# Scores of the first 128 queries as three products of rounded parts, in place of one product in full fp32

## The chip, the cores and the metric

The kernel runs on one core of one Trainium2 chip. A core has five engines that work side by side: TensorE (in the profile PE, with its weight loads as PEld), VectorE (DVE), ScalarE (ACT), GpSimd (POOL) and SyncE (SP). The metric is the device time of one execution in microseconds, taken as the median of several runs.

## The reference

The model is a trunk of two layers over 256 positions of 2048 features, with 32 heads of 128. The first layer (A) attends in chunks with a bias by relative distance, the second (B) to a shared key and value stream with a decay that forget gates set. Both have the same shape: a projection to queries, keys, values and a gate, scores, softmax, the weighted sum of the values, the gate, a projection back, a residual. The part that matters here, of layer B:

```python
for i in range(s // Q_BLOCK):               # Q_BLOCK = 128, s = 256
    q0 = i * Q_BLOCK
    end = q0 + Q_BLOCK
    sc = jnp.einsum('bqhd,bkhd->bhqk', q[:, q0:end], k[:, :end]).astype(jnp.float32) * scale
    decay = cum_logf_h[:, :, q0:end, None] - cum_logf_h[:, :, None, :end]
    causal = (q0 + jnp.arange(Q_BLOCK))[:, None] >= jnp.arange(end)[None, :]
    sc = jnp.where(causal[None, None], sc + decay, NEG_INF)
    p = jax.nn.softmax(sc, axis=-1).astype(v.dtype)
    outs.append(jnp.einsum('bhqk,bkhd->bqhd', p, v[:, :end]))
```

So the first 128 queries have scores with the first 128 keys alone, the other 128 queries with all 256. In layer A a chunk of 64 frames sees its own and the chunks before it, which the kernel computes in the same two blocks of 128 queries with a bias of -1e30 where nothing is seen. All is in fp32.

## The kernel before

**Products.** A product of fp32 values is made in one of two ways. In full fp32 it is one call of `pe.matmul`, which the profile shows as two matmul records and two weight loads. The other way splits both operands into a high part, rounded to the type `fp32r`, and a low part, the rounded remainder (`hi` and `lo`), and adds up three products: high by high, high by low, low by high. Every one of these is one record with one load. The large projections work so (`mm3`, L162: lines 164 to 166 are the three products of 512 columns), and so do most products of the attention (`dot3`, L330: lines 331 to 333).

**Order.** The weights of the projections come in blocks of 256 rows by 512 columns. `Feed` (L172) loads them by SP's queue, rounds the high part on ACT (L204) and takes the difference on DVE (L205). It keeps four blocks ready ahead of PE. The heads go in 16 groups of two in each layer, so there are 32 groups. For each group PE runs two units of eight blocks (`aqk` and `avg` in layer A, `bqg` and `bkv` in layer B), and the attention of a group is a generator (`attention`, L335) of which one piece is issued after a given block of the units that follow (`QK_STEPS` and its like; `drive`, L505). Instructions of an engine run in the order in which they are issued, and the buffers of tiles with the same tag are shared in turn, so that a new tile waits for the readers of the old one.

**Attention of one group.** The rows of q and k are transposed in squares of 32 on DVE and moved to their places by 16 DMAs that POOL issues (`turn`, L303). The tile that comes out, `qkZ` in the profile, has the features on the partitions. Then, as pieces of their own:

- `split` (L319) makes high and low parts on ACT (L326) and DVE (L327): of k for all 256 positions (`wideh`, `widel`), of q for the last 128 alone (`q1h`, `q1l`). The first 128 positions of q are copied in fp32 by ACT (L345) into `q0`, which takes the buffer of `oT`.
- The scores: `s1p`, the last 128 queries with all 256 keys, as three products per head with 256 columns each (L350, L351); and `s0p`, the first 128 queries with the first 128 keys, as one product in full fp32 per head with 128 columns (L353).
- Scale and bias on DVE (L360), the maximum (L361), the exponential on ACT (L363), first for `s1p`, then for `s0p`; then the gates are scaled, all is transposed again (`sgZ`), split (`wideh`, `widel` again), and multiplied with the values (`op`, L385 and L386).

At the start a few matmuls on a tile of zeros keep PE busy while the first data come (`heat`, L89).

Of the kernel before, what the change touches and what calls it, by code (L numbers as in the profile page):

```python
# [9 lines left out]
F32 = mybir.dt.float32  # L10
F32R = mybir.dt.float32r
BF16 = mybir.dt.bfloat16
AF = mybir.ActivationFunctionType
# [3 lines left out]
P = 128  # L17
S = 256
# [14 lines left out]
HG = 2  # L33
NG = H // HG
GC = HG * DH
UN = 512
KB = 2
SQ = 32
# [17 lines left out]
def r32(ap):  # L56
    return ap.bitcast(F32)
# [3 lines left out]
def trunk(ctx, tc, x, x_t, gains, a_w_in, a_rel, a_w_out, kv_w, f_w, f_b, b_w_in, b_w_out, final_norm, out):  # L61
    nc = tc.nc
    pe, act, dve, pool, sp = nc.tensor, nc.scalar, nc.vector, nc.gpsimd, nc.sync

    const = ctx.enter_context(tc.tile_pool(name="const", bufs=1))
    big = ctx.enter_context(tc.tile_pool(name="big", bufs=16))
    stream = ctx.enter_context(tc.tile_pool(name="stream", bufs=3))
    att = ctx.enter_context(tc.tile_pool(name="att", bufs=1))
# [5 lines left out]
    def bank(name):  # L74
        return ps_at.tile([P, 512], F32, name=name, tag="at")
# [12 lines left out]

    def heat(n):  # L89

        z = const.tile([P, P + UN], BF16, name="zeros")
        dve.memset(z, 0.0)
        ps = bank("heat")
        for i in range(n):
            pe.matmul(ps, z[:, :P], z[:, P:], start=i == 0, stop=i == n - 1)

    heat(HEAT)
    GA, GKV, GB = 0, KD, 2 * KD

# [203 lines left out]
    def turn(src, n, name):  # L303

        y = att.tile([P, NQ, n, SQ], F32, name=f"{name}Y", tag="Y")
        dve.transpose(y, src.rearrange("p n (j u) -> p j n u", u=SQ))  # L308
        z = att.tile([P, NQ, n, SQ], F32, name=f"{name}Z", tag="Z")
        for i in range(NQ):  # L310
            for j in range(NQ):
                pool.dma_start(out=z[j * SQ:(j + 1) * SQ, i], in_=y[i * SQ:(i + 1) * SQ, j])  # L312
        return z
# [2 lines left out]
        for t in range(NT):  # L316
            act.activation(dst[:, t], acc[t][:, c0:c1], AF.Copy, scale=rs[:, t:t + 1])

    def split(srcs, tag):  # L319

        n, nt = len(srcs), srcs[0].shape[1]
        hi = att.tile([P, n, nt * P], F32R, name=f"{tag}h", tag=f"{tag}h")
        lo = att.tile([P, n, nt * P], F32R, name=f"{tag}l", tag=f"{tag}l")
        for k, src in enumerate(srcs):
            h, l = (v[:, k].rearrange("p (t i u) -> p t i u", t=nt, u=SQ) for v in (hi, lo))
            act.activation(h, src, AF.Copy)  # L326
            dve.tensor_sub(l, src, r32(h))  # L327
        return hi, lo

    def dot3(out_, a, b, stop=True):  # L330
        pe.matmul(out_, a[0], b[0], start=True, stop=False)
        pe.matmul(out_, a[0], b[1], start=False, stop=False)
        pe.matmul(out_, a[1], b[0], start=False, stop=stop)

    def attention(g, biases, qk, vg, half, ocat):  # L335


        z = turn(qk.rearrange("p t (c d) -> p (t c) d", d=DH), NT * 2 * HG, "qk")
        bias1, bias0 = biases()
        qkT = z.rearrange("p i (t c) u -> p c t i u", t=NT)  # L340
        yield
        kh, kl = split([qkT[:, HG + i] for i in range(HG)], "wide")
        qh, ql = split([qkT[:, i, 1:] for i in range(HG)], "q1")
        q0 = att.tile([P, HG, P], F32, name="q0", tag="oT")
        act.activation(q0.rearrange("p h (i u) -> p h i u", u=SQ),  # L345
                       qkT[:, :HG, 0], AF.Copy)
        yield
        s1p = bank("s1p")[:, :].rearrange("p (i s) -> p i s", i=HG)
        s0p = bank("s0p")[:, :HG * P].rearrange("p (i s) -> p i s", i=HG)
        for i in range(HG):  # L350
            dot3(s1p[:, i], (qh[:, i], ql[:, i]), (kh[:, i], kl[:, i]))  # L351
        for i in range(HG):
            pe.matmul(s0p[:, i], q0[:, i], qkT[:, HG + i, 0], start=True, stop=True)  # L353
        NB = 1 + NT
        sg = att.tile([P, HG * NB + NT * HG, P], F32, name="sg", tag="R")
        sv = sg[:, :HG * NB].rearrange("p (i c) k -> p i (c k)", i=HG)
# [11 lines left out]
        c = small.tile([P, NT, HG], F32, name="csc")  # L368
# [7 lines left out]
        z = turn(sg, HG * NB + NT * HG, "sg")  # L376
        pT = z[:, :, :HG * NB].rearrange("p i (h c) u -> p h c i u", h=HG)
        gT = z[:, :, HG * NB:].rearrange("p i (t h) u -> p h t i u", t=NT)
        yield
        ph, pl = split([pT[:, i, :NT] for i in range(HG)], "wide")  # L380
        yield
        op = bank("op").rearrange("p (i s) -> p i s", i=HG)
# [5 lines left out]
        oT = att.tile([P, HG, S], F32, name="oT", tag="oT")  # L388
# [4 lines left out]
        lo = ocat.lo[h0 // BIG][:, h0 % BIG:h0 % BIG + HG, :]  # L393
# [87 lines left out]
    def side_a(g, accs):  # L481
        tb = att.tile([P, HG, S], F32, name="tb", tag="tb")
        for lo_, hi_, c0 in ((0, CHUNK, CHUNK), (CHUNK, P, 0)):
            sp.dma_start(out=tb[lo_:hi_, :, c0:], in_=bass.AP(
                tensor=a_rel.tensor, offset=a_rel.offset + g * HG * NREL + REL + 1 - P + lo_ + c0,
                ap=[[1, hi_ - lo_], [NREL, HG], [1, S - c0]]))

        def biases():
            pool.memset(tb[:CHUNK, :, :CHUNK], NEG)
            return tb[:, :, ::-1], tb[:, :, P - 1::-1]  # L490

        qk = rows(UN, "qk")
        evac_scaled(accs["qk"], 0, UN, rsA, qk)
        yield

        def vg():
            return accs["v"], accs["g"]

        yield from attention(g, biases, qk, vg, halfA, oA)
# [272 lines left out]
```

## Time and profile before

| | |
|---|---|
| median of 3 runs | 1859.43 us (1858.83 to 1859.74) |
| profiled execution | 1860.0 us |
| its span, first to last instruction | 1858.3 us |
| mean granted clock of TensorE | 0.996 |
| busy: PE, PEld | 1840.2 us, 1525.3 us |
| busy: DVE, ACT, POOL | 1123.8 us, 1008.2 us, 542.6 us |

A row of the profile that groups instructions has the line of the kernel, the engine, the operation, the tile written and the tiles read, the shape, the count, then the busy time in us, the mean duration of one in ns, and the engine's idle time before them with what ended it. `128*128 128x256` on a matmul is the size of the weights, then partitions by columns that stream. A row in order of time has the start in us, the duration in us, engine, line and operation; several alike are merged with their count, and the duration is then from the first start to the last end. A row of waits has who waited, for whom, the sum in us, how often, and the longest. A row by stretches of time has the stretch, its length, the busy time and count of PE, PEld, DVE, ACT and POOL, the granted clock, the share of the DMA engines and GB/s.

A matmul's record is as long as it takes from its start to its last result, and the next one starts before that. The time from one start to the next is therefore read from the order of time.

### The profile page before, as it was taken

The numbers are of one execution on the slowest core, as the hardware profiler recorded it, in microseconds if no ns is written. First come the engines' busy times: TensorE is split into PE (matmuls) and PEld (weight loads), VectorE is DVE, ScalarE is ACT, GpSimd is POOL, SyncE is SP. The second block draws the span as 40 slices with busy tenths as digits, with TensorE's granted clock in tenths as the row PEclk, the third lists the DMA queues.
The fourth block names the chain that finished last, engine by engine and source line by source line (L and its number), as shares of the span: only waits on it lengthen the run. The fifth ranks groups of instructions, "written<-read, shape, count | busy, mean of one in ns | idle before, by whom it ended". The sixth has DMA issues, their size and how long they took to land.

```text
span 1858.3 us, 25119 instructions
## 1 busy us (share of the span) xinstructions
PE 1840.2 (99%) x8395; PEld 1525.3 (82%) x8395; DVE 1123.8 (60%) x1450; ACT 1008.2 (54%) x1688; POOL 542.6 (29%) x1129
## 2 busy tenths in 40 slices
PE   8999999999999999999999999999999999999998
PEld 6888888888888888887888888888888888888886
DVE  6666656666666666555665666666665665655554
ACT  5555555555555555545555555555555655554443
POOL 0433333333333333111103333333333333333000
PEclk9999999999999999999999999999999999999999
DMA  8666666666676666666767666666666666676664
GB/s 281 216 216 210 212 214 219 214 208 217 215 212 210 217 215 212 208 218 222 230 185 220 209 216 215 216 217 213 214 214 218 214 213 213 212 235 214 207 203 161
DMA packets 141970, 398.43 MB, mean 214 GB/s; under 512 B 31088, under 2 KB 35472, under 8 KB 141456
## 3 DMA queue, kind: packets, MB, share of 16 engines
q1 hardware_dynamic: 106816, 356.35, 60.3%
q0 software_dynamic: 34304, 39.39, 6.6%
q8 instruction: 67, 1.10, 0.2%
q10 hardware_dynamic: 720, 1.07, 0.2%
q14 instruction: 63, 0.52, 0.1%
HBM read 353.15 MB, written 4.23 MB: 192 GB/s over the span
## 4 chain that ended last, share of the span: by engine, by line
PE 88%; DMA 5%; DVE 2%; POOL 2%; ACT 2%; issue 1%; SPq 0%; ACTq 0%; POOLq 0%; DVEq 0%
PE avg_acc L164 6%; PE bqg_acc L164 6%; PE bqg_acc L166 6%; PE bqg_acc L165 6%; PE avg_acc L165 6%; PE avg_acc L166 6%; PE bkv_acc L164 5%; PE bkv_acc L165 5%; PE bkv_acc L166 5%; PE aqk_acc L166 5%; PE aqk_acc L164 5%; PE aqk_acc L165 5%; PE bo_acc L166 3%; PE bo_acc L165 3%; PE bo_acc L164 3%; DMA sgZ<-sgY 2%
## 5 line engine op out<-in xcount | busy, mean ns | idle before, releaser
L312 POOL DMA_DIRECT2D sgZ<-sgY x512 | 250.5, 497 | 467.9 <-DVE sgY L308 410.1
L312 POOL DMA_DIRECT2D qkZ<-qkY x512 | 251.0, 497 | 379.4 <-DVE vl L405 97.3
L205 DVE TENSOR_TENSOR avg_lo<-avg_raw,avg_hi 128x1024 fp32r<-128x1024 f32 x128 | 156.5, 1223 | 130.3 <-ACT avg_hi L204 130.2
L205 DVE TENSOR_TENSOR bqg_lo<-bqg_raw,bqg_hi 128x1024 fp32r<-128x1024 f32 x128 | 156.6, 1223 | 129.4 <-ACT bqg_hi L204 129.4
L204 ACT ACTIVATE bqg_hi<-bqg_raw 128x1024 fp32r<-128x1024 f32 x128 | 135.4, 1058 | 143.2 <-PE bqg_acc L166 85.1
L204 ACT ACTIVATE avg_hi<-avg_raw 128x1024 fp32r<-128x1024 f32 x128 | 135.3, 1057 | 141.3 <-PE avg_acc L166 84.0
L205 DVE TENSOR_TENSOR aqk_lo<-aqk_raw,aqk_hi 128x1024 fp32r<-128x1024 f32 (+1 forms) x129 | 155.3, 1211 | 88.3 <-ACT aqk_hi L204 88.2
L164 PE MATMUL aqk_acc<-aqk_hi,xTh 128*128 128x512 f32 x512 | 202.2, 396 | 3.3 <-ACT xTh L142 3.0
L205 DVE TENSOR_TENSOR bkv_lo<-bkv_raw,bkv_hi 128x1024 fp32r<-128x1024 f32 x128 | 155.3, 1219 | 77.0 <-ACT bkv_hi L204 76.7
L166 PE MATMUL aqk_acc<-aqk_hi,xTl 128*128 128x512 f32 x512 | 200.6, 392 | 1.1 <-DVE xTl L143 1.1
L165 PE MATMUL aqk_acc<-aqk_lo,xTh 128*128 128x512 f32 x512 | 200.6, 392 | 1.1 <-DVE aqk_lo L205 1.1
L164 PE MATMUL bkv_acc<-bkv_hi,xkvh 128*128 128x512 f32 x512 | 201.1, 393 | 0.0
L164 PE MATMUL avg_acc<-avg_hi,xTh 128*128 128x512 f32 x512 | 200.7, 392 | 0.0
L164 PE MATMUL bqg_acc<-bqg_hi,xbh 128*128 128x512 f32 x512 | 200.7, 392 | 0.0
L166 PE MATMUL bqg_acc<-bqg_hi,xbl 128*128 128x512 f32 x512 | 199.5, 390 | 0.0
L166 PE MATMUL bkv_acc<-bkv_hi,xkvl 128*128 128x512 f32 x512 | 199.5, 390 | 0.0
L166 PE MATMUL avg_acc<-avg_hi,xTl 128*128 128x512 f32 x512 | 199.4, 389 | 0.0
L165 PE MATMUL bqg_acc<-bqg_lo,xbh 128*128 128x512 f32 x512 | 199.3, 389 | 0.0
L165 PE MATMUL avg_acc<-avg_lo,xTh 128*128 128x512 f32 x512 | 199.3, 389 | 0.0
L165 PE MATMUL bkv_acc<-bkv_lo,xkvh 128*128 128x512 f32 x512 | 199.2, 389 | 0.0
L204 ACT ACTIVATE aqk_hi<-aqk_raw 128x1024 fp32r<-128x1024 f32 (+1 forms) x129 | 134.8, 1050 | 86.2 <-PE aqk_acc L166 46.0
L204 ACT ACTIVATE bkv_hi<-bkv_raw 128x1024 fp32r<-128x1024 f32 x128 | 134.6, 1057 | 72.8 <-PE bqg_acc L166 41.9
(193 smaller groups left out, 3451.8 us busy)
## 6 DMA issues: line engine op xcount, KB each, us to landing
avg_raw<-in_a_w_in SPq DMA_DIRECT2D x128, 512.0 KB, 4.2
bqg_raw<-in_b_w_in SPq DMA_DIRECT2D x128, 512.0 KB, 4.2
bkv_raw<-in_kv_w SPq DMA_DIRECT2D x128, 512.0 KB, 4.2
aqk_raw<-in_a_w_in SPq DMA_DIRECT2D x127, 512.0 KB, 4.1
ao_raw<-in_a_w_out SPq DMA_DIRECT2D x64, 512.0 KB, 4.3
bo_raw<-in_b_w_out SPq DMA_DIRECT2D x64, 512.0 KB, 4.1
sgZ<-sgY POOLq DMA_DIRECT2D x512, 40.0 KB, 3.9
qkZ<-qkY POOLq DMA_DIRECT2D x512, 32.0 KB, 3.6
```

The costliest lines, as they stand in the source:

```text
L164: pe.matmul(acc[t], lhs.h(k)[:, ts], hi, start=k == 0, stop=False)
L165: pe.matmul(acc[t], lhs.h(k)[:, ts], lo, start=False, stop=False)
L166: done.append(pe.matmul(acc[t], lhs.l(k)[:, ts], hi, start=False, stop=k == nk - 1))
L204: act.activation(hi[:, j], raw[:, j], AF.Copy)
L205: self.splits.append(dve.tensor_sub(lo[:, j], raw[:, j], r32(hi[:, j])))
L312: pool.dma_start(out=z[j * SQ:(j + 1) * SQ, i], in_=y[i * SQ:(i + 1) * SQ, j])
```

## The change

The scores of the first 128 queries are made like those of the last: three products of rounded parts for each head, with 128 columns. For this, q is split over all its 256 positions (`qh`, `ql`), and the fp32 copy `q0` goes. The first 128 columns of the rounded q and k serve `s0p`, the last 128 of q and all of k serve `s1p`. The low part of q takes the buffer of `oT`, where `q0` was (`split` has an argument for it), and the zeros of the warm-up take the buffer of the gates, `gs`, in place of one of their own.

```diff
     def heat(n):
-        z = const.tile([P, P + UN], BF16, name="zeros")
+        z = att.tile([P, P + UN], BF16, name="zeros", tag="gs")
...
-    def split(srcs, tag):
+    def split(srcs, tag, low=None):
         n, nt = len(srcs), srcs[0].shape[1]
         hi = att.tile([P, n, nt * P], F32R, name=f"{tag}h", tag=f"{tag}h")
-        lo = att.tile([P, n, nt * P], F32R, name=f"{tag}l", tag=f"{tag}l")
+        lo = att.tile([P, n, nt * P], F32R, name=f"{tag}l", tag=low or f"{tag}l")
...
         kh, kl = split([qkT[:, HG + i] for i in range(HG)], "wide")
-        qh, ql = split([qkT[:, i, 1:] for i in range(HG)], "q1")
-        q0 = att.tile([P, HG, P], F32, name="q0", tag="oT")
-        act.activation(q0.rearrange("p h (i u) -> p h i u", u=SQ),
-                       qkT[:, :HG, 0], AF.Copy)
+        qh, ql = split([qkT[:, i] for i in range(HG)], "q", "oT")
         yield
...
-        for i in range(HG):
-            dot3(s1p[:, i], (qh[:, i], ql[:, i]), (kh[:, i], kl[:, i]))
-        for i in range(HG):
-            pe.matmul(s0p[:, i], q0[:, i], qkT[:, HG + i, 0], start=True, stop=True)
+        for s_, t, n in ((s1p, 1, S), (s0p, 0, P)):
+            for i in range(HG):
+                dot3(s_[:, i], *((h[:, i, c], l[:, i, c]) for h, l, c in
+                                 ((qh, ql, slice(t * P, (t + 1) * P)), (kh, kl, slice(0, n)))))
```

## The prediction

> **What bounds the kernel now.** I read the head of the profile page first, then the waits of PE, then the busy time by stage.
>
> ```profile
> span 1858.3 us, 25119 instructions
> PE 1840.2 (99%) x8395; PEld 1525.3 (82%) x8395; DVE 1123.8 (60%) x1450; ACT 1008.2 (54%) x1688; POOL 542.6 (29%) x1129
> ...
> PE 88%; DMA 5%; DVE 2%; POOL 2%; ACT 2%; issue 1%; SPq 0%; ACTq 0%; POOLq 0%; DVEq 0%
> ```
>
> ```profile
> PE aqk_acc L164 <- ACT xTh L142: 3.0, 1, 3.0
> ...
> PE aqk_acc L165 <- DVE aqk_lo L205: 1.1, 3, 0.5
> ...
> PE ao_acc L165 <- DVE ao_lo L205: 0.8, 1, 0.8
> PE op L331 <- ACT wideh L326: 0.6, 2, 0.3
> ...
> PE cp L626 <- DVE f_l L615: 0.2, 1, 0.2
> ```
>
> ```profile
> 45.00:750.00 705.00, 704.65 (x3238) 586.27 (x3237) 431.63 (x550) 383.88 (x641) 244.61 (x509) 1.00 0.68 213
> ...
> 1000.00:1690.00 690.00, 689.28 (x3176) 574.51 (x3175) 425.95 (x539) 399.82 (x720) 247.10 (x510) 1.00 0.68 216
> ```
>
> PE is busy for 1840.2 of 1858.3 us. Its waits fill nine rows (the first, the last and the three that a later step needs are shown), all small, and none belongs to the scores. In the two long stretches that hold nearly all of the attention, the first number after the length is PE's busy time: 704.65 of 705 us and 689.28 of 690. The granted clock there is 1.00. So every nanosecond that the change adds to or takes from the PE's stream moves the end by as much, and work on the other engines counts only where it makes PE wait.
>
> A busy PE may hide slow and quick instructions alike, since a record's duration (275 ns for a product of 128 columns) is a latency that overlaps the next record. What counts is the pitch: the time from one record's start to the next one's. So the rest is read from the order of time, and the first question is which of the two pipelined streams, weight loads (PEld) or matmuls (PE), sets that pitch.
>
> **What the edited products cost now.** These are records by form, and then the last of the 32 groups of two heads in order of time.
>
> ```profile
> L353 PE MATMUL s0p<-qkZ,q 128*128 128x128 f32 x128 | 19.6, 275 | 0.0
> ...
> L353 PEld LDWEIGHTS s0p<-qkZ,q 128*128 128x128 f32 x128 | 17.1, 191 | 0.0
> L331 PEld LDWEIGHTS s1p<-wideh,q1h 128*128 128x128 f32 x64 | 12.2, 190 | 1.3
> ...
> L332 PEld LDWEIGHTS s1p<-widel,q1h 128*128 128x128 f32 x64 | 12.2, 190 | 1.2
> ...
> L590 PEld LDWEIGHTS zp<-xkvl,fwh 128*32 128x32 f32 x16 | 1.7, 108 | 0.1
> ```
>
> ```profile
> 1693.92 0.39 PE L164 MATMUL bo_acc<-bo_hi,oBh 128*128 128x512 f32 x1
> ...
> 1694.60 0.28 PE L331 MATMUL s1p<-wideh,q1h 128*128 128x256 f32 x1
> ...
> 1695.31 0.61 PE L353 MATMUL s0p<-qkZ,q 128*128 128x128 f32 x4
> 1695.68 0.47 PE L164 MATMUL bo_acc<-bo_hi,oBh 128*128 128x512 f32 x1
> 1695.99 0.39 PE L165 MATMUL bo_acc<-bo_lo,oBh 128*128 128x512 f32 x1
> ```
>
> There are 64 full-fp32 products (32 heads in two layers) and 128 records: each product is two matmuls with two loads. From 1693.92 three matmuls of 512 columns (L164, L165, L166) go by until 1694.60, so one takes 0.227 us. Six products of rounded parts with 256 columns take from 1694.60 to 1695.31: 0.71/6 = 0.118 us each. From the first fp32 record to L165 are 0.68 us; without the 0.227 us of the L164 between them, 0.453 us is left for four records, 0.113 us each, 0.227 us for a product.
>
> Is this 0.113 us the matmul's or the load's? The cumulative sum of the gates answers that, with six fp32 records of only 32 columns against 128-wide weights:
>
> ```profile
> 973.67 0.38 PE L626 MATMUL cp<-f_l,triu 128*128 128x32 f32 x2 [0.17 <-DVE f_l L615]
> 973.88 0.39 PE L626 MATMUL cp<-f_l,ones 128*128 128x32 f32 x2
> 974.11 0.39 PE L626 MATMUL cp<-f_l,triu 128*128 128x32 f32 x2
> 974.33 0.48 PE L164 MATMUL bkv_acc<-bkv_hi,xkvh 128*128 128x512 f32 x1
> ```
>
> ```profile
> 973.64 0.30 PEld L626 LDWEIGHTS cp<-f_l,triu 128*128 128x128 f32 x2 [0.56 <-issue]
> ...
> 974.30 0.19 PEld L164 LDWEIGHTS bkv_acc<-bkv_hi,xkvh 128*128 128x128 f32 x1
> ```
>
> Six records take 0.66 us, six loads 0.66 us: 0.110 us each, although only a quarter as many columns stream as in s0p. A load of 128 fp32 weights thus takes about 0.110 us of its own stream. The durations agree: 190 ns for 128 weights and 108 ns for 32 make (190 - 108)/96 = 0.85 ns a weight, 109 ns for 128, and the loads of rounded weights (L331 and L332 of s1p) last as long as those of fp32. A narrow product on its own weights therefore can't have a pitch below the load's.
>
> **The change part by part.**
>
> (1) The products. Two fp32 products of a group (four records, 0.453 us) give way to two times three products of rounded parts: six records, each with a load of 128 weights. `dot3` uses the high part of q twice in a row, but s1p does so today, and both lines there have 64 loads of their own, so all six loads stay. The trace has no rounded product with fewer than 256 columns, so its pitch must be bounded. From below: if the matmul's stream alone set it, by the slope (0.227 - 0.118)/256 = 0.426 ns a column, it is 0.118 - 128 x 0.426 = 0.064 us. From above: half the columns should not take longer than the 0.118 us of the 256-wide product, as long as the rate per column holds. I take 0.112 us, the row of the gates and of s0p itself, because these have the same load and no longer stream than it; the 0.064 us would need a load quicker than any of this size in the trace. That makes 2 records more at 0.112 us, +0.224 us a group and +7.2 us over 32 groups. By 0.118 us all six take 0.708 us, +0.255 us a group, +8.2 us; by 0.064 us they take 0.384 us, -0.069 us a group, -2.2 us.
>
> The Trainium skill, "TensorE: Matmul & The Clock Gate", section "Back-to-back issue gap", speaks against this: it gives 81 ns for each matmul of 128 columns in a stream of load and matmul pairs. By that figure six would take an estimated 0.486 us and the change would cost only 1.1 us in all; the trace's 0.110 us with 32 columns disagrees.
>
> (2) The splits. Both heads' q is now rounded over 256 columns and not 128, and the copy at L345 goes.
>
> ```profile
> L326 ACT ACTIVATE wideh<-qkZ 128x256 fp32r<-128x256 f32 x64 | 23.3, 410 | 69.7 <-DMA qkZ<-qkY 69.7
> ...
> L326 ACT ACTIVATE q1h<-qkZ 128x128 fp32r<-128x128 f32 x64 | 15.8, 294 | 0.0
> ...
> L345 ACT ACTIVATE q<-qkZ 128x256 f32<-128x256 f32 x32 | 12.8, 402 | 0.0
> ```
>
> ```profile
> L327 DVE TENSOR_TENSOR widel<-qkZ,wideh 128x256 fp32r<-128x256 f32 x64 | 24.4, 421 | 45.1 <-ACT wideh L326 45.1
> ...
> L327 DVE TENSOR_TENSOR q1l<-qkZ,q1h 128x128 fp32r<-128x128 f32 x64 | 15.6, 285 | 0.0
> ```
>
> ACT: 2 x (410 - 294) - 402 = -170 ns a group. DVE: 2 x (421 - 285) = +272 ns a group, 8.7 us in all on an engine that is 60% busy. The low part is ready 0.27 us later. What covers it is the distance to the product that reads it. In the group with the least distance but one, and in the first:
>
> ```profile
> 240.21 0.49 DVE L327 TENSOR_TENSOR q1l<-qkZ,q1h 128x128 fp32r<-128x128 f32 x2
> ...
> 243.84 0.28 PE L333 MATMUL s1p<-wideh,q1l 128*128 128x256 f32 x1
> ```
>
> ```profile
> 58.51 0.49 DVE L327 TENSOR_TENSOR q1l<-qkZ,q1h 128x128 fp32r<-128x128 f32 x2
> ...
> 59.00 0.28 PE L333 MATMUL s1p<-wideh,q1l 128*128 128x256 f32 x1
> ```
>
> In the fifth group the low parts end at 240.70 and are read at 243.84, over 3 us later. The other 30 have more. Only the first group has them done (59.00) as the PE gets there; I put down 0.2 us, once. Queued behind the longer split on DVE are the low parts of the next weight blocks (L205), four blocks ahead of PE; they take up 0.27 us, since PE waits for such a part only in the first blocks and by 0.8 us in the first output projection. If that cover were gone everywhere, it would cost 32 x 0.27 = 8.7 us.
>
> (3) Later readers and buffers. The scores of the first 128 queries end 0.22 us later. Their reader comes late anyway:
>
> ```profile
> 1697.92 0.41 DVE L360 SCALAR_TENSOR_TENSOR sg<-s0p,d 128x256 f32<-128x256 f32 x1
> ```
>
> It starts 1.9 us after the PE has left s0p (1695.99), since DVE does the other 128 queries first. The low part of q takes the buffer of oT, as q0 did, so it waits for the same readers of the group before; the zeros of the warm-up move into the buffer of the gates, which nothing writes before the first group's second unit is done. No DMA is added or moved, and the transposed tile comes free earlier. All this: 0. The two waits of op (0.6 us) may grow by what the exponentials come later, at most 0.3 us each.
>
> **The sum.** +7.2 + 0.2 = +7.4 us. The profiled run took 1860.0 us (span 1858.3 and 1.7 around it): 1867.4. The median, 1859.43, is 0.6 below that run, which gives 1866.8 us, +0.4%. Its own range runs from 1865.8 (all six at the 0.109 us of the durations: 0.654 us, +0.201 us a group, +6.4 us, and no stall) to 1868.4 (0.118 us: +8.2, the first group's 0.2 and 0.6 for op).
>
> **The rivals.**
>
> A, loads hidden. If rounded weights come through faster than fp32 ones when matmuls are short, the stream sets the pitch: 0.064 us, -2.2 us, 1857.2. For it: at 256 and 512 columns nothing shows that rounded loads hinder. Against: their durations equal those of fp32 weights (190 and 191 ns). It decides below a pitch of 0.453/6 = 0.0755 us; there the change stops costing, and up to (0.453 + 3.7/32)/6 = 0.095 us it stays within 0.2%. The 81 ns of the Trainium skill would fall between these two points and make it 1860.5.
>
> B, passes count. If the price is the array's passes, three replace four: 0.227/4 = 0.057 us less a product, x64 = -3.6 us, 1855.8. The Trainium skill, "FP8 and Floating Point Precision", section "TensorE Precision Notes", counts four passes for true FP32. Against it stands L626: a quarter of the columns at the same pitch.
>
> C, narrow rounded products lose their rate. If under 256 columns each costs what a full-fp32 product does (0.227 us), six take 1.36 us, +0.91 us a group, +29.0 us: 1888.4. Nothing in the trace speaks for or against, since all its rounded products have 256 or 512 columns.
>
> D, the change doesn't do what it says: the repeated high part of q isn't loaded again, four loads as now, no change, 1859.6. Against: the 64 loads on each of the lines 331 and 332.
>
> E, the late split starves PE in all groups: +7.2 + 8.7, 1875.3. Against: the 3 us of cover.
>
> **How the numbers follow.** The forecast 0.74; A 0.10, B 0.04, C 0.06, D 0.03, E 0.03. From 1865.8 to 1868.4 leaves 0.26 out, so the range goes on to A and D: 1857.0 to 1869.0, with 0.13 outside. Of no change I speak up to 0.2%, 3.7 us, about what a measurement of this kernel can tell. Slower are the forecast, C and E, 0.83; A, D and most of B are within it, 0.14; the rest of B, faster, 0.03.
>
> **What would show it.** Right: 192 records of s0p with 192 loads of 128x128, in order of time 0.90 us from the first of them to L165 (now 0.68), PE busier by some 7 us, its waits still about 9, L345 gone from ACT and DVE's splits of q 8.7 us longer. Wrong: a pitch near 0.07 (A) or 0.23 (C), 128 loads (D), or a wait of PE for a split of q beyond the first group (E). A pitch of 0.112 with no longer time would mean that PE isn't the bound, and my reading of its busy time fails.

## The result and the profile after

The changed kernel takes 1870.96 us (median of 4 runs, 1867.66 to 1875.45); the kernel before takes 1859.13 us beside it (4 runs, 1857.07 to 1859.74). The ratio is 1.0065, with a 95% interval from 1.0051 to 1.0078. So the change makes the kernel slower, as forecast, but by about 12 us and not by 7.4, and the median lies above the range (the lowest of its four runs, 1867.66 us, lies in it). The profiled execution took 1872.6 us with a span of 1870.8 us, 12.5 us more than the span before.

The head of the profile page, and the first and the last row of PE's waits (who waited, for whom, sum in us, times, longest):

```profile
span 1870.8 us, 25069 instructions
PE 1848.3 (99%) x8459; PEld 1535.1 (82%) x8459; DVE 1137.7 (61%) x1450; ACT 1003.6 (54%) x1656; POOL 544.0 (29%) x1129
...
PE 90%; DMA 3%; DVE 2%; POOL 2%; issue 1%; ACT 1%; SPq 0%; ACTq 0%; POOLq 0%; DVEq 0%
```

```profile
PE op L331 <- ACT wideh L326: 5.1, 4, 2.2
...
PE cp L623 <- DVE f_l L612: 0.2, 1, 0.2
```

PE is still the bound. It has 64 records more and is busy for 8.1 us more. The wait that has grown most is that of `op`, the product of the exponentials with the values, for the high part of its transposed weights: from 0.6 us in 2 waits to 5.1 us in 4. The one at the start for `xTh` grew from 3.0 to 4.4 us, while some small ones fell. All rows of PE's waits add up to 13.2 us, against 9.0 before.

The records of the edited part by form:

```profile
L331 PE MATMUL s0p<-wideh,qh 128*128 128x128 f32 x64 | 15.9, 248 | 0.0
...
L333 PEld LDWEIGHTS s0p<-wideh,ql 128*128 128x128 f32 x64 | 12.3, 192 | 0.0
...
L327 DVE TENSOR_TENSOR ql<-qkZ,qh 128x256 fp32r<-128x256 f32 x64 | 24.1, 417 | 0.0
...
L326 ACT ACTIVATE qh<-qkZ 128x256 fp32r<-128x256 f32 x64 | 22.7, 402 | 0.0
```

The change does what it says. Each of the lines 331 to 333 has 64 records of 128 columns for `s0p`, and each has 64 loads of its own.

**What a group costs where nothing disturbs it.** PE's records in order of time (start, duration in us), after the change, from the scores of one group to those of the next:

```profile
1333.55 0.28 PE L331 MATMUL s1p<-wideh,qh 128*128 128x256 f32 x1
...
1334.27 0.22 PE L331 MATMUL s0p<-wideh,qh 128*128 128x128 f32 x1
...
1334.89 0.45 PE L164 MATMUL bkv_acc<-bkv_hi,xkvh 128*128 128x512 f32 x1
1335.17 0.39 PE L165 MATMUL bkv_acc<-bkv_lo,xkvh 128*128 128x512 f32 x1
...
1337.67 0.39 PE L164 MATMUL bkv_acc<-bkv_hi,xkvh 128*128 128x512 f32 x1
...
1379.68 0.28 PE L331 MATMUL s1p<-wideh,qh 128*128 128x256 f32 x1
```

And the same view of the kernel before, for the same group:

```profile
1325.92 0.28 PE L331 MATMUL s1p<-wideh,q1h 128*128 128x256 f32 x1
...
1326.63 0.61 PE L353 MATMUL s0p<-qkZ,q 128*128 128x128 f32 x4
...
1327.31 0.39 PE L165 MATMUL bkv_acc<-bkv_lo,xkvh 128*128 128x512 f32 x1
...
1329.85 0.39 PE L164 MATMUL bkv_acc<-bkv_hi,xkvh 128*128 128x512 f32 x1
...
1371.86 0.28 PE L331 MATMUL s1p<-wideh,q1h 128*128 128x256 f32 x1
```

From the first record of `s0p` to L165 it is now 0.90 us (1334.27 to 1335.17), before 0.68 us: the forecast's +0.22. But the whole period of the group grows from 45.94 us (1325.92 to 1371.86) to 46.13 us (1333.55 to 1379.68), by only 0.19 us. The rest was in the matmuls that follow: the eleven from L165 on took 2.54 us before (1327.31 to 1329.85) and take 2.50 us now (1335.17 to 1337.67). After the full-fp32 records the next wide matmuls ran a little slower, and after these six rounded ones they don't. It isn't fp32 alone that makes them slower: after four rounded records, and after two, the same eleven take 2.52 us (the runs with two products and with one, below). What does is open. Over 32 groups 0.187 us (the difference before rounding, mean of the undisturbed groups) make 6.0 us.

**Where the other 6.5 us are.** The first score product of each group marks the time. The records of `s1p<-wideh,qh` in each layer (count, minimum, median and maximum duration in ns, first and last start in us; the last is the second head of the last group), of the kernel before and then of the changed one:

```profile
L331 PE MATMUL s1p<-wideh,q1h x32: 277/280/283, 58.8 to 751.4; 128*128 128x256 f32 x32
...
L331 PE MATMUL s1p<-wideh,q1h x32: 277/280/283, 1003.3 to 1695.0; 128*128 128x256 f32 x32
```

```profile
L331 PE MATMUL s1p<-wideh,qh x32: 277/280/283, 60.2 to 754.8; 128*128 128x256 f32 x32
...
L331 PE MATMUL s1p<-wideh,qh x32: 277/280/283, 1005.3 to 1707.1; 128*128 128x256 f32 x32
```

| stretch | before | after | difference |
|---|---|---|---|
| start to the first score | 58.8 | 60.2 | +1.4 |
| layer A, first to last score | 692.6 | 694.6 | +2.0 |
| to the first score of layer B | 251.9 | 250.5 | -1.4 |
| layer B, first to last score | 691.7 | 701.8 | +10.1 |
| to the end | 163.3 | 163.7 | +0.4 |

Fifteen periods in each layer should cost 15 x 0.187 = 2.8 us more. Layer A has less than that, layer B 7.3 us beyond it. There it sits in two of its groups: the second to start in layer B takes 50.67 us and the thirteenth 50.32 us, where before they took 46.97 and 46.99 us. So 46.13 is exceeded by 4.5 and 4.2 us, 45.94 was exceeded by 1.0 each. Here is what PE does at the end of the first of the two, in order of time (in brackets the idle time and what ended it), and by stretches (length, busy time and count of PE, PEld, DVE, ACT, POOL, then the granted clock):

```profile
1074.36 0.39 PE L166 MATMUL bkv_acc<-bkv_hi,xkvl 128*128 128x512 f32 x1
1076.94 0.39 PE L331 MATMUL op<-wideh,vh 128*128 128x256 f32 x1 [2.19 <-ACT wideh L326]
...
1079.75 0.63 PE L165 MATMUL bqg_acc<-bqg_lo,xbh 128*128 128x512 f32 x1
```

```profile
1074.56:1077.97 3.41, 1.15 (x5) 0.66 (x5) 0.76 (x2) 1.50 (x3) 0.00 (x0) 1.00 0.16 61
1077.97:1081.38 3.41, 3.41 (x12) 3.01 (x13) 3.21 (x5) 2.72 (x7) 0.00 (x0) 0.50 0.23 67
```

PE waits 2.19 us for the split of the transposed exponentials. At 1077.97, 1.03 us after the wait has ended, the granted clock falls to 0.50 for 3.41 us, and the wide matmul at 1079.75 lasts 0.63 us where it otherwise takes 0.39. (In the other group it falls 0.45 us after the wait, and the last section says what the two have in common.) At half speed 3.4 us do the work of 1.7. So the wait costs nearly twice its length, and PE's busy time hides the second half of it.

**Why `op` waits.** DVE in the same group, before and then after, from the scores to the transposition of the exponentials (`sgY`):

```profile
1050.23 0.69 DVE L360 SCALAR_TENSOR_TENSOR sg<-s1p,cb 128x512 f32<-128x512 f32 x1 [1.18 <-PE s1p L333]
1050.84 0.41 DVE L360 SCALAR_TENSOR_TENSOR sg<-s0p,d 128x256 f32<-128x256 f32 x1
1051.17 1.00 DVE L361 TENSOR_REDUCE nm<-sg 128x2 f32<-128x512 f32 x2
1052.09 1.21 DVE L205 TENSOR_TENSOR bkv_lo<-bkv_raw,bkv_hi 128x1024 fp32r<-128x1024 f32 x1
...
1055.89 1.51 DVE L308 STREAM_TRANSPOSE sgY<-sg 128x1280 f32<-128x1280 f32 x1
```

```profile
1052.42 0.69 DVE L357 SCALAR_TENSOR_TENSOR sg<-s1p,cb 128x512 f32<-128x512 f32 x1 [1.19 <-PE s1p L333]
1053.03 1.22 DVE L205 TENSOR_TENSOR bkv_lo<-bkv_raw,bkv_hi 128x1024 fp32r<-128x1024 f32 x1
1054.16 0.68 DVE L358 TENSOR_REDUCE nm<-sg 128x2 f32<-128x512 f32 x1
1054.76 0.41 DVE L357 SCALAR_TENSOR_TENSOR sg<-s0p,d 128x256 f32<-128x256 f32 x1
...
1058.89 1.51 DVE L308 STREAM_TRANSPOSE sgY<-sg 128x1280 f32<-128x1280 f32 x1
```

Before, both scores and both maxima came in one piece. Now the low part of a weight block (L205, 1.22 us) stands between the first score and the first maximum, and the second score comes after that. No line of the diff says so: the planner, which lays the order of DVE's instructions, laid it anew for the changed program, in all 16 groups of layer B. (Before, only the last of them had this order. In layer A the order changed too, to score, maximum, score, maximum, but with no weight part between, and there the transposition starts 5.67 us after the first score in nearly all groups, as before.) The transposition starts 6.47 us after the first score (1052.42 to 1058.89), not 5.66 us (1050.23 to 1055.89). Then 16 transfers follow, issued by POOL, and the rounding on ACT. That rounding in the same group, before and after:

```profile
1072.20 0.72 ACT L326 ACTIVATE wideh<-sgZ 128x256 fp32r<-128x256 f32 x2 [4.17 <-DMA sgZ<-sgY]
```

```profile
1076.47 0.72 ACT L326 ACTIVATE wideh<-sgZ 128x256 fp32r<-128x256 f32 x2 [6.06 <-DMA sgZ<-sgY]
```

It comes 24.05 us after the first score and not 21.97. PE, on the other hand, arrives at `op` 22.33 us after it (1076.94 - 2.19 - 1052.42). Of the 2.08 us that were lost, 0.81 are DVE's; the other 1.27 came up behind it: 0.53 until POOL had issued the last of the transfers, where it waits for earlier ones of the same tile, and 0.74 from there to the rounding. POOL's issues in order of time, after:

```profile
1065.40 4.40 POOL L312 DMA_DIRECT2D sgZ<-sgY  x9 [2.72 <-issue]
1070.13 0.50 POOL L312 DMA_DIRECT2D sgZ<-sgY  x1 [0.33 <-DMA sgZ<-sgY]
1071.40 0.50 POOL L312 DMA_DIRECT2D sgZ<-sgY  x1 [0.77 <-DMA sgZ<-sgY]
```

The gap of 2.72 us in POOL's issues is there in the kernel before as well (2.75 us in this group); both kernels have such a gap, of 2.7 to 3.3 us, in the `sgZ` transfers of four groups out of 32, and these two are among them. All four already exceeded the 45.94 us before, by 0.6 to 1.0 us, and exceed 46.13 us now, the two in layer A by 1.0 and 1.4 us. So it is in these groups above all that the slack runs out.

### The profile page after: what moved, and what is told of

The parts are those of the page before. It is cut to its first block, busy times and chain, and to the rows that moved or that the text cites. A ratio compares the mean times of both kernels' runs of the same rounds, so it can differ in the third digit from the quotient of the medians.

```text
span 1870.8 us, 25069 instructions
## 1 busy us (share of the span) xinstructions
PE 1848.3 (99%) x8459; PEld 1535.1 (82%) x8459; DVE 1137.7 (61%) x1450; ACT 1003.6 (54%) x1656; POOL 544.0 (29%) x1129
## 4 chain that ended last, share of the span: by engine, by line
PE 90%; DMA 3%; DVE 2%; POOL 2%; issue 1%; ACT 1%; SPq 0%; ACTq 0%; POOLq 0%; DVEq 0%
PE avg_acc L164 6%; PE avg_acc L166 6%; PE avg_acc L165 6%; PE bqg_acc L164 6%; PE bqg_acc L165 6%; PE bqg_acc L166 6%; PE aqk_acc L164 5%; PE aqk_acc L166 5%; PE aqk_acc L165 5%; PE bkv_acc L164 5%; PE bkv_acc L166 5%; PE bkv_acc L165 5%; PE ao_acc L165 3%; PE bo_acc L164 3%; PE ao_acc L164 3%; PE ao_acc L166 3%
## 5 line engine op out<-in xcount | busy, mean ns | idle before, releaser
L205 DVE TENSOR_TENSOR avg_lo<-avg_raw,avg_hi 128x1024 fp32r<-128x1024 f32 x128 | 156.4, 1223 | 131.3 <-ACT avg_hi L204 131.0
L205 DVE TENSOR_TENSOR bqg_lo<-bqg_raw,bqg_hi 128x1024 fp32r<-128x1024 f32 x128 | 156.6, 1223 | 130.5 <-ACT bqg_hi L204 130.4
L205 DVE TENSOR_TENSOR aqk_lo<-aqk_raw,aqk_hi 128x1024 fp32r<-128x1024 f32 (+1 forms) x129 | 156.2, 1215 | 92.9 <-ACT aqk_hi L204 92.8
L164 PE MATMUL aqk_acc<-aqk_hi,xTh 128*128 128x512 f32 x512 | 201.9, 395 | 5.0 <-ACT xTh L142 4.4
L164 PE MATMUL bqg_acc<-bqg_hi,xbh 128*128 128x512 f32 x512 | 201.5, 394 | 0.0
L165 PE MATMUL aqk_acc<-aqk_lo,xTh 128*128 128x512 f32 x512 | 200.6, 392 | 0.8 <-DVE aqk_lo L205 0.8
L164 PE MATMUL avg_acc<-avg_hi,xTh 128*128 128x512 f32 x512 | 200.7, 392 | 0.0
L164 PE MATMUL bkv_acc<-bkv_hi,xkvh 128*128 128x512 f32 x512 | 200.4, 391 | 0.0
L165 PE MATMUL bqg_acc<-bqg_lo,xbh 128*128 128x512 f32 x512 | 200.0, 391 | 0.0
L165 PE MATMUL avg_acc<-avg_lo,xTh 128*128 128x512 f32 x512 | 199.3, 389 | 0.0
L165 PE MATMUL bkv_acc<-bkv_lo,xkvh 128*128 128x512 f32 x512 | 199.2, 389 | 0.0
L205 DVE TENSOR_TENSOR bkv_lo<-bkv_raw,bkv_hi 128x1024 fp32r<-128x1024 f32 x128 | 155.8, 1224 | 59.2 <-ACT bkv_hi L204 58.0
```

The costliest lines, as they stand in the source:

```text
L164: pe.matmul(acc[t], lhs.h(k)[:, ts], hi, start=k == 0, stop=False)
L165: pe.matmul(acc[t], lhs.h(k)[:, ts], lo, start=False, stop=False)
L205: self.splits.append(dve.tensor_sub(lo[:, j], raw[:, j], r32(hi[:, j])))
```

## The experiments

Two terms are to be told apart: the loads (6.0 us, in each group) and the order (about 6 us, in a few groups). The theory: a record's price is its load, and the late split comes of the new order on DVE, not of the products themselves. Rivals: columns or the longer splits set the price; or the stall comes with the additional PE time. `tc.issue_after(x)` in the diffs below keeps what stands in its block behind the instruction x in the planner's order.

### The first queries' products over all 256 keys

The rounded products of `s0p` take 256 columns in place of 128; the other 128 are read by no one.

```diff
-        s0p = bank("s0p")[:, :HG * P].rearrange("p (i s) -> p i s", i=HG)
-        for s_, t, n in ((s1p, 1, S), (s0p, 0, P)):
+        s0w = bank("s0p")[:, :].rearrange("p (i s) -> p i s", i=HG)
+        s0p = s0w[:, :, :P]
+        for s_, t, n in ((s1p, 1, S), (s0w, 0, S)):
```

> The changed kernel, but the products for the first 128 queries run over the first 256 keys and not 128 (the second half is computed and never read). Theory 'the weight load sets the pitch': the six records of a group go from 0.112 to 0.118-0.120 us each, the same as those of s1p, so from the first s0p record to L165 0.95 us and not 0.91, and the whole is 1 to 2 us slower than the changed kernel (1870.96), about 1872.5. Rival 'the columns that stream set it': 6 x 128 x 0.426 ns = 0.33 us more a group, +10.5 us, about 1881.5.

Measured: 1872.4 us (4 runs, 1870.17 to 1874.7), ratio to the kernel before 1.0065 [1.0052, 1.0079], the same as the change itself. PE in order of time, from the first of the six records to what follows:

```profile
1103.73 0.28 PE L331 MATMUL s0p<-wideh,qh 128*128 128x256 f32 x1
...
1104.45 0.40 PE L164 MATMUL bkv_acc<-bkv_hi,xkvh 128*128 128x512 f32 x1
```

Six take 0.72 us, 0.120 us each with twice the columns, and the undisturbed group takes 46.19 us, 0.07 us more than after the change. So what a product of 128 columns costs is almost wholly not its columns. The time is the expected one.

### Two of the three products, and one

Of `s0p` alone, first the product of q's high part with k's low part is left out, then also the one of q's low part with k's high part.

```diff
-        for s_, t, n in ((s1p, 1, S), (s0p, 0, P)):
-            for i in range(HG):
-                dot3(s_[:, i], *((h[:, i, c], l[:, i, c]) for h, l, c in
-                                 ((qh, ql, slice(t * P, (t + 1) * P)), (kh, kl, slice(0, n)))))
+        q1, q0, k0 = slice(P, S), slice(0, P), slice(0, P)
+        for i in range(HG):
+            dot3(s1p[:, i], (qh[:, i, q1], ql[:, i, q1]), (kh[:, i], kl[:, i]))
+        for i in range(HG):
+            pe.matmul(s0p[:, i], qh[:, i, q0], kh[:, i, k0], start=True, stop=False)
+            pe.matmul(s0p[:, i], ql[:, i, q0], kh[:, i, k0], start=False, stop=True)
```

> The changed kernel with the term high part of q by low part of k left out of the scores of the first 128 queries: four records and four loads a group, as many as the full-fp32 products had; all else, the order of the instructions on DVE too, as in the changed kernel. Theory 'load pitch, plus PE waits for the transposed exponentials (wideh before op) that came with the later and reordered softmax': the load term goes (-7.2 us), the waits of op and the clock drops behind them stay in part: 1860 to 1866. Rival 'all of the 11.8 us came from the products': 1859 or less. Rival 'the products cost nothing, it is all order and waits': 1868 or more.

```diff
-            pe.matmul(s0p[:, i], qh[:, i, q0], kh[:, i, k0], start=True, stop=False)
-            pe.matmul(s0p[:, i], ql[:, i, q0], kh[:, i, k0], start=False, stop=True)
+            pe.matmul(s0p[:, i], qh[:, i, q0], kh[:, i, k0], start=True, stop=True)
```

> The changed kernel with only the product of the two high parts for the first 128 queries (both cross terms left out): two records and two loads a group; the planner's order on DVE is that of before. Theory 'each record of 128 columns costs a load, 0.10 us': the period of an undisturbed group falls by another 0.20 us to 45.73 us, and the whole is 1851 to 1854. Rival 'not the number of loads': a period above 45.85 us, 1856 or more.

Measured: with two 1863.08 us (12 runs, 1860.39 to 1869.18), ratio 1.0017 [1.0007, 1.0026]; with one 1851.4 us (5 runs, 1850.15 to 1852.9), ratio 0.9944 [0.9932, 0.9957]. The undisturbed groups have periods of 46.127 us (six records), 45.927 (four) and 45.707 (two): 0.100 and 0.110 us for each record that goes, near the 45.73 us expected for two. A record and its load go together here, so these runs don't tell the load's price from a fixed price of a record. That rival is open, and one place speaks for it: in the kernel before the two records of `cT` (L632, 128 columns on weights of only 32) are 0.108 us apart, although their loads last 0.09 us and the weight loads sit idle for 0.14 us before the second. Four rounded records cost as much as four of full fp32 (45.940). The kernel with two products kept the new order on DVE and a part of its stalls:

```profile
PE op L331 <- ACT wideh L326: 3.9, 3, 1.7
```

Its undisturbed groups are no longer than those of before, so its 0.2% more lie outside of them, and this wait is the largest thing there; the kernel with one product, which makes as many calls as the full-fp32 kernel, has the old order and 1.3 us of this wait. Both times are as expected.

### The splits alone

The kernel before with q split over 256 positions, the low part in the buffer of `oT`, the zeros in that of the gates, and the products of before; `q0` gets its own buffer.

```diff
...
-        qh, ql = split([qkT[:, i, 1:] for i in range(HG)], "q1")
-        q0 = att.tile([P, HG, P], F32, name="q0", tag="oT")
+        qh, ql = split([qkT[:, i] for i in range(HG)], "q", "oT")
+        q0 = att.tile([P, HG, P], F32, name="q0")
...
+        q1 = slice(P, S)
...
-            dot3(s1p[:, i], (qh[:, i], ql[:, i]), (kh[:, i], kl[:, i]))
+            dot3(s1p[:, i], (qh[:, i, q1], ql[:, i, q1]), (kh[:, i], kl[:, i]))
```

> The products of before (full fp32 for the first 128 queries, with their fp32 copy of q, now in a buffer of its own), with the longer split of q, the low part of q in the buffer of oT and the zeros in the buffer of the gates, as in the changed kernel; DVE's order is that of before. Theory 'the split and the buffers are hidden': 1859 to 1860, the waits of PE near 9 us. Rival 'the split or the buffers make the rest of the loss': 1862 to 1866, with waits of PE for wideh or for a split of q.

Measured: 1858.22 us (12 runs, 1856.18 to 1863.74), ratio 0.9994 [0.9984, 1.0004], the period of a group 45.94 us, `op` waits 0.8 us in 2. The order on DVE is that of before. So neither the longer splits nor the moved buffers cost anything that can be measured, and they don't cause the new order.

### The scores one block earlier

In the changed kernel the splits and scores are issued one block earlier; then the same in the kernel before.

```diff
-QK_STEPS = {0: 1, 6: 1, 7: 2}
+QK_STEPS = {0: 1, 5: 1, 6: 2}
...
-B1_STEPS = {0: 1, 6: 1, 7: 2}
+B1_STEPS = {0: 1, 5: 1, 6: 2}
```

> The changed kernel with the scores and the split before them issued one block of weights (2.7 us) earlier in both layers, so that the transposed exponentials come 2.7 us earlier for the products that wait for them. Theory 'six loads cost 0.187 us more a group (the period of an undisturbed group: 46.127 against 45.940 us), and the rest is PE's wait for wideh before op in a few groups with the clock drop behind it': no waits of op over 0.3 us, no clock drop in the middle, 1864 to 1866. Rival 'the rest is something else in the changed kernel': 1868 or more.

> The kernel before with scores and split one block earlier, as in the changed kernel with the earlier scores. Theory: the kernel before loses little to the waits of op (0.6 us in its profile, groups of 46.6 to 47.0 us against 45.94), so 0.5 to 3 us faster: 1856.5 to 1859. Rival 'earlier scores bring new waits for the splits': 1860 or more.

Measured: the changed kernel 1867.11 us (7 runs, 1863.55 to 1868.38), ratio to the kernel before 1.0025 [1.0014, 1.0037]; the kernel before with the same edit 1859.53 us (11 runs, 1856.51 to 1860.96), ratio 0.9991 [0.9982, 1.0000]. Two of PE's waits in the changed kernel with it:

```profile
PE s1p L331 <- ACT qh L326: 1.4, 2, 0.9
...
PE op L331 <- ACT wideh L326: 1.0, 2, 0.6
```

With some slack more the wait of `op` shrinks from 5.1 to 1.0 us, no clock is lost in the groups, and their period stays at 46.13 us. This is so although the new order stays, in both layers: what counts is when the exponentials arrive. The earlier scores now wait for their own split (1.4 us). Against the kernel before, measured beside it (1860.55 us), the changed kernel is 6.6 us slower and not 11.8, so some 5 us are won, but not all that the order cost. The time lies between its two expectations (up to 1866, or 1868 and more), and the longest wait of `op` is 0.6 us and not under 0.3. The kernel before gains nothing that is clear, less than the 0.5 to 3 us expected.

### The order of DVE put back, in two steps

First the low parts of the weight blocks are kept behind the last maximum on DVE.

```diff
...
-                self.splits.append(dve.tensor_sub(lo[:, j], raw[:, j], r32(hi[:, j])))
+                with tc.issue_after(last[0].ins) if last else ExitStack():
+                    self.splits.append(dve.tensor_sub(lo[:, j], raw[:, j], r32(hi[:, j])))
...
-            dve.tensor_reduce(nm[:, t], s_, axis=AX.X, op=OP.max, negate=True)
+            last[:] = [dve.tensor_reduce(nm[:, t], s_, axis=AX.X, op=OP.max, negate=True)]
```

> The changed kernel with one thing pinned: the low parts of the weights (L205) that are traced after the softmax's maxima are kept behind these on DVE, as they stood before the change. Theory 'in layer B the weight split that slipped between the two scores delays the transposed exponentials, PE then waits for wideh before op, and a wait of 2 us is followed by a stretch at half clock': the waits of op fall to under 1 us, no clock drop in the middle, and only the load term is left: 1864 to 1866. Rival 'the order on DVE does not matter': 1868 to 1873 as the changed kernel, with the same waits.

Measured: 1877.03 us (6 runs, 1873.08 to 1879.1), ratio 1.0087 [1.0074, 1.01]. It was slower than the change, against the expectation. The wait of `op`, then ACT and DVE in order of time in a group of layer B:

```profile
PE op L333 <- ACT wideh L328: 7.0, 6, 1.7
```

```profile
1290.88 0.69 ACT L648 ACTIVATE d<-cb,cum 128x128 f32<-128x128 f32 x2 [2.06 <-DMA cb<-cumd]
1291.48 1.27 ACT L373 ACTIVATE sg<-gs,csc 128x128 f32<-128x128 f32 x4
```

```profile
1292.78 1.51 DVE L310 STREAM_TRANSPOSE sgY<-sg 128x1280 f32<-128x1280 f32 x1 [3.55 <-ACT sg L373]
```

In 15 of the 16 groups of layer B no weight part stands between the scores any more (the order is score, maximum, score, maximum), but the planner moved something else: on ACT the biases of the next group (L648) now stood ahead of the scaling of the gates (L373) and waited 2.06 us for a transfer, and the transposition waited 3.55 us for the gates. So the second step also keeps the biases behind the gates:

```diff
...
-                act.activation(sg[:, HG * NB + t * HG + i], gs[:, t, i * DH:(i + 1) * DH], AF.Copy,
-                               scale=c[:, t, i:i + 1])
+                gate[:] = [act.activation(sg[:, HG * NB + t * HG + i], gs[:, t, i * DH:(i + 1) * DH], AF.Copy,
+                                          scale=c[:, t, i:i + 1])]
...
-                act.activation(d0[:, i], cb[:, i, :P], AF.Identity, bias=cum[:, 0, h:h + 1], scale=-1.0)
-                act.activation(cb[:, i], cb[:, i], AF.Identity, bias=cum[:, 1, h:h + 1], scale=-1.0)
+                with tc.issue_after(gate[0].ins):
+                    act.activation(d0[:, i], cb[:, i, :P], AF.Identity, bias=cum[:, 0, h:h + 1], scale=-1.0)
+                    act.activation(cb[:, i], cb[:, i], AF.Identity, bias=cum[:, 1, h:h + 1], scale=-1.0)
```

> As the run with the pinned weight splits on DVE, and on ACT the biases of the next group (which wait for a DMA) pinned behind the scaling of the gates, so that neither engine puts foreign work ahead of the second transpose. Theory: the transpose of the exponentials starts no later than 5.6 us after the last score product also in layer B, the waits of op fall under 2 us in sum and the whole is 1864 to 1868. Rival 'the order on ACT and DVE does not decide it': 1871 or more, with waits of op as in the changed kernel.

Measured: 1862.29 us (11 runs, 1861.22 to 1866.27), ratio 1.0009 [1.0001, 1.0018]. DVE in order of time, and the first and last of PE's nine waits:

```profile
1099.15 0.69 DVE L360 SCALAR_TENSOR_TENSOR sg<-s1p,cb 128x512 f32<-128x512 f32 x1 [0.49 <-PE s1p L336]
...
1104.24 1.51 DVE L311 STREAM_TRANSPOSE sgY<-sg 128x1280 f32<-128x1280 f32 x1 [1.35 <-ACT sg L374]
```

```profile
PE aqk_acc L166 <- ACT xTh L142: 3.2, 1, 3.2
...
PE cp L626 <- DVE f_l L615: 0.2, 1, 0.2
```

The transposition starts 5.09 us after the first score, none of the nine rows names `op`, and the clock isn't lost in the groups. The products are those of the change, all six, and the undisturbed group still takes 46.13 us. So order alone is worth some 10 us here (1.0065 against 1.0009). It is not the order of before but an earlier one: in layer B the transposition mostly starts 4.83 us after PE's last score record, in the kernel before 5.60 us, in the changed kernel 6.24 us (medians). The time is lower than expected, too: groups of this kernel exceed their 46.13 us by 2.1 us in all, those of the profile before their 45.94 us by 5.4 us. It wins back 3.3 us of the 6.0 there.

### The order alone, with the products of before

The opposite: in the kernel before, the low part of a weight block is set between the two scores, in both layers. For this the next weight block is prepared at that place (`feed.prepare()`), its rounding on ACT too. The products are untouched.

```diff
-            dve.scalar_tensor_tensor(s_, sp_, SCALE, bias, op0=OP.mult, op1=OP.add)
+            if not t:
+                feed.prepare()
+            with ExitStack() if t else tc.issue_after(feed.splits[-1].ins):
+                dve.scalar_tensor_tensor(s_, sp_, SCALE, bias, op0=OP.mult, op1=OP.add)
```

> The kernel before, its products and its splits of q untouched, with one order imposed on DVE: a low part of the weights (L205) goes between the scores of the last and of the first 128 queries, as the planner of the changed kernel has it in layer B (here in both layers). Theory 'that order alone makes PE wait before op': waits of op of several us in sum, perhaps a clock drop in the middle, the period of undisturbed groups unchanged at 45.94 us, and 1862 to 1868. Rival 'it is the products': 1859 to 1861 and waits of op near 0.6 us.

Measured: 1893.89 us (5 runs, 1888.88 to 1898.11), ratio 1.0178 [1.0158, 1.0199]. The wait of `op`:

```profile
PE op L331 <- ACT wideh L326: 16.2, 14, 2.7
```

The time is far above the 1862 to 1868 us expected. The wait grows from 0.6 to 16.2 us, the clock falls to one half in four places in the groups, and the least period of a group stays at 45.94 us. The edit delays more than the change did (the transposition comes 8.11 us after the last score record in layer A and 6.41 in layer B, medians, where the change has 5.43 and 6.24), so the size is not that of the change; but it shows that order on these engines makes this wait and this loss of clock, with no product changed.

### The exponentials first, in the kernel before

All weight splits are kept behind the gates on ACT and the transposition on DVE, to see if the slack of `op` has anything to give. The edit also issues the scaling of the gates and the transposition ahead of the next block of weights, and keeps the biases behind the gates as above.

```diff
-PV_STEPS = {0: 1, 6: 1, 7: 2}
+PV_STEPS = {6: 1, 7: 2}
...
-                act.activation(hi[:, j], raw[:, j], AF.Copy)
-                self.splits.append(dve.tensor_sub(lo[:, j], raw[:, j], r32(hi[:, j])))
+                with tc.issue_after(gate[0].ins) if gate else ExitStack():
+                    act.activation(hi[:, j], raw[:, j], AF.Copy)
+                with tc.issue_after(last[0].ins) if last else ExitStack():
+                    self.splits.append(dve.tensor_sub(lo[:, j], raw[:, j], r32(hi[:, j])))
...
```

> The kernel before, the other way: the scaling of the gates and the transpose of the exponentials are issued before the next block of weights and pinned ahead of it on ACT and DVE, so that the transposed exponentials come some 2 us earlier. Theory: the waits of op (0.6 us, and some of the disturbed groups of 46.6 to 47.0 us) go, which is worth 1 to 2.5 us: 1857 to 1859.5. Rival 'the weight splits pushed behind it come too late for PE': new waits on hi or lo parts, 1861 or more.

Measured: 1928.94 us (4 runs, 1923.42 to 1932.36), ratio 1.037 [1.035, 1.039], against the expectation.

```profile
PE op L338 <- DVE widel L333: 26.3, 30, 0.9
```

The transposition does come earlier (5.27 us after the first score, not 5.67), but now `op` waits for the low part of the exponentials in nearly every group: on DVE a delayed weight split of 1.23 us (L209) stands between the low parts of the two heads (read in one group of layer B). What was moved away from one place of the queue came back ahead of the next reader.

## Why the prediction was right and where it failed

**The bound: right, but with no term for the clock.** PE is busy for 1848.3 of 1870.8 us, and what was added to its stream moved the end. The sum took the clock of 1.00 as given; two stretches at half clock cost 1.7 us each.

**Step (1), the products: right in the pitch, too large by a sixth.** From the first of the six records to L165 are 0.90 us, as forecast; five of their pitches are 0.109 to 0.115 us, and the first, 0.061, is made up by a longer L164 behind them. There are 192 loads. Products of twice the columns cost 0.120 us, and taking records away gives back 0.100 to 0.110 us each. That it is the load that sets this, and not a fixed price of a record, the prediction took from six records and six loads with the same pitch, which doesn't tell them apart. The Trainium skill, "TensorE: Matmul & The Clock Gate", section "Back-to-back issue gap", with 81 ns for such a pair, doesn't fit these 32-bit operands. What was mis-sized is what the fp32 products had cost: "0.453 us is left for four records" counts up to the next L165 only, and eleven wide matmuls behind it were slower by 0.04 us in all, which they no longer are. So the term is 0.187 us a group, 6.0 us, not 7.2. That tail stood in the trace before, though nothing there told that it would go; with two and four rounded records a part of it is still there.

**Step (2), the splits: right.** DVE's split of q takes 64 x 417 ns in place of 64 x 285, +8.5 us (forecast 8.7); ACT has 4.6 us less (forecast 5.4); the run with the splits alone shows no cost. PE waits for no split of q beyond the first group.

**Step (3), later readers: this is where it failed.** "The two waits of op (0.6 us) may grow by what the exponentials come later, at most 0.3 us each." This took the order of DVE from the trace before and moved it by 0.22 us as a whole. But the order is laid by a planner, and with six records in place of four it was laid differently: the split of a weight block slipped in between the scores, the transposition came 0.8 us later, and `op` had little slack to begin with, as its two waits of before should have told. Seven of the 30 periods before were in fact 0.4 to 1.0 us too long at `op`, more than its row of waits shows, as the records behind a late `op` are further apart as well. The wait grew by 4.5 us and took the clock with it. That both follow from when the exponentials arrive, and this from the order, is shown by three runs together: with the order mended (to one earlier than before) they are gone at the same products, with the scores a block earlier nearly so, and with the order alone they appear with the products of before. PE's added time isn't needed for it: with two products per head the group is no longer than before, and `op` still waits 3.9 us. Why the planner chose as it did is not shown: the splits alone left the order as it was, one rounded product per head too, and two per head changed it, which points to the number of products; and which part of the 2.08 us in the stalled group is due to DVE's delay and which to the meeting of transfers wasn't tried.

**The rivals.** A and B ended with the pitch, C with it too, D with the 192 loads. E came near in time (1875.3) by luck: it named the right sort of event, a late split that starves PE, but in all groups and at the wrong place: at the scores, where there are 3 us of cover, and not at `op`.

**The numbers.** 6.0 us for the loads and 6.6 us for the stalls, as the disturbed groups exceed their period by 11.9 us now and by 5.4 us before, make the 12.5 us of the two profiles within 0.1; the start (+1.4) and the stretch between the layers (-1.4) cancel. The range ended at 1869.0 because the stall had a bound of 0.6 us, from an order that the change didn't keep. Of the signs listed, "its waits still about 9" was the one that showed it: they were 13.2 (1.4 of the 4.2 us more lie at the start).

The only version clearly below the kernel before is the one with a single rounded product (0.9944), which leaves out two of the three terms. The splits alone and the earlier scores in the kernel before lie at 0.9994 and 0.9991, with intervals that reach 1.

## What to carry to other kernels

Price narrow matmuls on their own weights by the record with its load (0.10 to 0.11 us here), not by the columns, and measure the cost of a replaced product on the whole period, not on its records alone. Where a planner lays the order, an edit on one engine may reorder the others: look for the dependency with the least slack in the profile before (a wait that is short but there) and give it a bound of its own, worth one foreign instruction in its chain, not the shift of the edit alone. Putting an order back by pinning one instruction may only move the disturbance to the next queue, so read the order of each engine in the chain after it.

## What the runs showed of the hardware beyond what was expected

**When the clock is lost.** After waits of PE of 2.19 and 2.02 us the clock went to one half for 3.41 us; in the kernel with two products it did so after one of 1.40 us, and not after one of 1.74 us; in the kernel with the order half put back, not after 1.73 us. So the length of the wait alone doesn't decide. Its place counts, too: in each of these traces all changes of the clock lie whole steps of 3.413 us apart (1077.97 and 1589.97 us after the change: 512.00 us, 150 steps), and a stretch at half clock in the groups is one or two steps long. What counts is how long PE sits idle within the one step that ends where the clock falls. Between the first 35 and the last 12 us of all twelve traces (idle times above 0.1 us, steps at full clock), every step with 1.65 us or more of idle PE was followed by half clock (eight of them, 2.19 and 2.02 us among these), and none with 1.33 us or less. The wait of 1.74 us fell across two steps, 1.51 and 0.23 us, that of 1.73 us with 0.62 and 1.10 us, that of 1.40 us into one. Between 1.40 and 1.51 us three steps lost the clock and two didn't, and what decides there is open. The Trainium skill, "TensorE: Matmul & The Clock Gate", section "Why this matters for your kernels", warns of gaps above about 3 us; the drops here came after shorter ones.

**Narrow products.** A rounded product on its own weights takes 0.112 us with 128 columns and 0.120 us with 256, so the second 128 columns are nearly free.
